# Weight-sum transfers tied to the weight stream, and a fifth raw tile in the last mixed stretch

## The chip, the cores and the metric

The kernel runs on one core of one Trainium2 chip. The metric is the device time of one execution in microseconds (us). Before the change, three runs gave a median of 2760.9 us (2760.19 to 2761.02).

## What is computed

The reference is a two-layer encoder over 272 tokens (16 learned meta tokens and 256 others) of width 2048, all in float32. Cut to what matters:

```
h = RMSNorm(x);  [q|k|v|f|ga|gf] = h @ w_in
a = attention(q, k, v) @ w_attn_br        # per-head norms, rotary
s = Re(2-D DFT(f)) @ w_four
x = x + (sigmoid(ga)*a + sigmoid(gf)*s) @ w_out
x = x + (silu(conv3(RMSNorm(x) @ w_up_gate)) * (RMSNorm(x) @ w_up_val)) @ w_down
```

There are few tokens and many weights, so the kernel is one long stream of weights past a small set of activations. Each float32 product is made of three TensorE products: an operand is split into a rounded high half and the remainder, and high*high, high*low and low*high are added.

## The kernel before, in words

**The stream.** `order` (from line 145) lists all weight groups, and `chunks` all pieces of 512 KB (128 partitions x 1024 float32) in the order of use. For each chunk, `load_raw` (line 198) issues a load on SP's DMA queue into one of `RAW` = 4 raw tiles. `split_w` (line 231) then writes the high half `wh` on ACT (line 237) and the low half `wl` on DVE (line 239); each has three buffers, and a raw tile is free when its `wl` is written. `next_split` (line 275) hands the pair to the matmuls, and splitting runs `LOOK` = 2 chunks ahead. `group` (line 282) does one weight group: 24 matmuls for a chunk, at lines 308 to 310. A chunk is eight 128x128 weight blocks; after every second block, thus four times a chunk, it calls `step` (line 250).

**Side work.** `step` advances generators that were pushed for norms, attention, the Fourier branch and others; what they emit is placed between the matmuls. `step` also counts down a slow generator, `weight_sums` (line 488), first by 120 steps and then by whatever it yields, which is 28. A planner then orders the instructions on each engine by their dependences, their costs and their place in the program; with `tc.keep_in_program_order` an instruction keeps its place.

**The weight sums.** The last layer's down projection treats the first 32 of its 44 feature tiles as a 2x2 block product with seven instead of eight block products (`PRODUCTS`, line 38). Four of them need sums of weight blocks, which stand in DRAM as `ft`. `weight_sums` builds these with DMAs from DRAM to DRAM, issued by GpSimd (POOL): eight rounds of eight transfers of 1 MB. Four of each round copy (line 501), and four add to what is there (line 503). They read only inputs and `ft` itself. `ft` is first read when the products that use it start, late in the last layer.

**Other users of POOL's queue.** POOL runs its queue in order. It also computes the reciprocal square roots of the norms (`pow_half`, line 446, instruction at line 448): `tok` for a token norm, `rk` and `rq` for the keys' and queries' head norms. In the head of the program, layer 0's first groups (`first_groups`, from line 351; matmuls at lines 376 to 378) run the first eight chunks. Their results wait in PSUM for `rstdB`, which comes from `tok` through `ps_nb` (line 527); the keys wait for `rk` through `dk` and `ps_kb` (lines 883 and 886).

**The mixed stretch.** A chunk of the seven products has six matmuls of 512 columns (line 1273), and there are 112 such chunks (`pchunks`). They are mixed into the stream: `due` (line 181) spreads 58 of them over the 48 chunks of the last six up and gate groups of layer 1, and 54 over the 24 chunks of the tail (matmuls at line 1334). `make` (line 1245) prepares the activations for a unit of four product chunks as a pair of halves, `opnd`, in three buffers; it is called at the first chunk of a unit, for the unit after the next.

Of the kernel before, what the change touches and what calls it, by code (L numbers as in the profile page):

```python
# [10 lines left out]
F32 = mybir.dt.float32  # L11
F32R = mybir.dt.float32r
# [4 lines left out]
P = 128  # L17
# [15 lines left out]
CW = 4  # L33
MG = 2
# [98 lines left out]
def encoder_kernel(ctx, tc, xT, params, consts, bmat, cfold, csign, w_fl, w_f64c, w_in, w_abr, w_four, w_f64, w_out, w_up, w_down, w_dn, w_dt, out):  # L133
    nc = tc.nc
    per = ctx.enter_context(tc.tile_pool(name="per", bufs=1))
    wp = ctx.enter_context(tc.tile_pool(name="wp", bufs=3))
# [41 lines left out]
    prods = {0: w_dn[0, 0:NQ], 1: w_dn[0, NQ:KS], 2: w_dn[1, NQ:KS], 3: ft[3], 4: ft[0], 5: ft[1], 6: ft[2]}  # L178
    pchunks = [(prods[p][i], CW) for p in PRODUCTS for i in range(NQ)]
    n_up, n_tail = (FT - KS) // MG * 2 * KT // CW, len(TAIL_ORDER) * (FT - KS) // 2  # L180
    due = lambda t: 58 * t // n_up if t <= n_up else min(58 + (len(pchunks) - 58) * (t - n_up) // (n_tail - 2), len(pchunks))
    chunks, folded, mix = [], set(), {}
    t, done = 0, 0
    for key, chs in order:
        for j, ch in enumerate(chs):
            if key[0] == 1 and (key[1] == "t" or key[1] in ("ug", "uv") and key[2] >= KS // MG):
                mix[key, j] = due(t) - done
                chunks += pchunks[done:due(t)]
                done = due(t)
                t += 1  # L190
            if key[:2] == (0, "s"):
                folded.add(len(chunks))
            chunks.append(ch)
    st = {"raw": 0, "fetch": 0, "next": 0, "grp": 0}
    raws, splits = {}, {}
    RAW, LOOK = 4, 2

    def load_raw(i):
        src, n = chunks[i]
        r = wp.tile([P, CW, MG * P], F32, tag="raw", name=f"raw{i}", bufs=RAW)  # L200
        nc.sync.dma_start(r, src)
        raws[i] = r

    todo = []

    def advance(upto):
        while st["raw"] < min(upto + RAW, len(chunks)):
            load_raw(st["raw"])
            st["raw"] += 1
        while st["fetch"] < min(upto, len(chunks)):  # L210
            i = st["fetch"]
            if i in folded:
                todo.append((i, lambda i=i: fold_w(i)))
            for a in (0, 2) if i <= 3 else (0,):
                todo.append((i, lambda i=i, a=a: split_w(i, a, a + 2 if i <= 3 else CW)))
            st["fetch"] += 1
# [8 lines left out]
    def fold_w(i):  # L225
        r = wp.tile([P, CW, MG * P], F32, tag="wpm", name=f"wpm{i}", bufs=1)
        for o, op in ((0, ALU.add), (2, ALU.subtract)):
            nc.vector.tensor_tensor(r[:, o:o + 2], raws[i][:, 0:2], raws[i][:, 2:4], op=op)
        raws[i] = r

    def split_w(i, a, b, parts="hl"):
        if i not in splits:
            splits[i] = tuple(wp.tile([P, CW, MG * P], F32R, tag=t, name=f"{t}{i}") for t in ("wh", "wl"))
        h, lo = splits[i]
        r = raws[i]
        if "h" in parts:
            nc.scalar.copy(h[:, a:b], r[:, a:b])  # L237
        if "l" in parts:
            nc.vector.tensor_tensor(lo[:, a:b], r[:, a:b], h[:, a:b].bitcast(F32), op=ALU.subtract)  # L239
            if b == CW:  # L240
                del raws[i]
# [167 lines left out]
    small = ctx.enter_context(tc.tile_pool(name="small", bufs=4))  # L409
# [78 lines left out]
    def weight_sums():  # L488
        rows = lambda ap: ap.rearrange("k p c m -> (k p) (c m)")
        for j in range(NQ // 2):  # L490
            a, b = 2 * j, 2 * j + 2
            dst = lambda q: rows(ft[q, a:b])
            w = lambda h, k: rows(w_dn[h, NQ * k + a:NQ * k + b])
            for ops in ((((0, w(0, 0)), (2, w(1, 1)), (3, w(0, 1))), None),
                        (((0, w(1, 0)), (2, w(1, 0))), ALU.add),
                        (((1, None),), None),
                        (((1, w(1, 1)),), ALU.add),
                        (((3, dst(1)),), ALU.add)):
                for q, src in ops[0]:
                    if ops[1] is None:  # L500
                        nc.gpsimd.dma_start(dst(q), dst(0) if src is None else src)
                    else:
                        nc.gpsimd.dma_start(dst(q), src, accum_op=ops[1], max_dma_last_dim=4096)
                    yield 28

    def norm_stats(holder, gap=0):
# [29 lines left out]
    for l in range(DEPTH):  # L536
        last = l == DEPTH - 1
        lo = 14 if last else 0
# [4 lines left out]
        with tc.tile_pool(name=f"mix{l}", bufs=1) as mp:  # L543
# [524 lines left out]
            for i in range(4):  # L1068
# [8 lines left out]
                elif i == 0:  # L1077
                    until(hold, "vt")
                    until(hold, "fold")
                    for t_, n in ((qH, "q1"), (qL, "q2")):  # L1080
                        t = mp.tile([P, NH, T], F32R, tag=n, name=n)
# [25 lines left out]
            for half in range(2):  # L1107
                mH = mL = None
                for kind, i in BRANCH_ORDER[half]:
# [19 lines left out]
                    else:  # L1129
# [7 lines left out]
                        for m in range(MG):  # L1137
                            k = 2 * j + m
                            t_, h_ = tha[i][:, m, lo:T], mH[:, k, lo:T]
# [13 lines left out]
        with tc.tile_pool(name=f"ffn{l}", bufs=1) as fp:  # L1153
# [48 lines left out]
            if last:  # L1202
# [11 lines left out]
                def act(k, n, tk):  # L1214
                    k0, t_ = acts[k >= KX]
                    return t_[:, k - k0:k - k0 + n, tk]
# [24 lines left out]
                def products():  # L1241
                    units = [(p, q) for p in PRODUCTS for q in range(NQ // 4)]
                    made = {}

                    def make(u):
                        if u >= len(units):
                            return
                        p, q = units[u]
                        k1, k2 = 4 * q, NQ + 4 * q
                        s = asum[:, k1:k1 + 4]  # L1250
                        if p == 5:
                            nc.vector.tensor_tensor(s, s, act(k1, 4, tk1), op=ALU.subtract)
                        if p == 2:
                            nc.vector.tensor_tensor(s, s, act(k2, 4, tk1), op=ALU.add)
                        v = {0: act(k1, 4, tk1), 1: act(k2, 4, tk1), 3: act(k2, 4, tk2), 6: act(k1, 4, tk2)}.get(p, s)
                        t_ = fp.tile([P, 2, 4, P], F32R, tag="opnd", name="opnd", bufs=3)
                        split_to(t_[:, 0], t_[:, 1], v)
                        made[u] = t_

                    make(0)  # L1260
                    make(1)
                    usum = wp.tile([P, CW, MG * P], F32, tag="wpm", name="usum", bufs=1).rearrange("p c m -> p (c m)")
                    for n, p in enumerate(PRODUCTS):
                        ps = [psum.tile([P, 512], F32, tag="aux", name=f"ps_p{p}") for _ in range(2)]
                        for i in range(NQ):
                            u = (n * NQ + i) // 4
                            if i % 4 == 0:
                                make(u + 2)
                            wh, wl = (w.rearrange("p c m -> p (c m)") for w in next_split())
                            a, b = made[u][:, 0, i % 4], made[u][:, 1, i % 4]  # L1270
                            for x, w in ((a, wh), (b, wh), (a, wl)):
                                for h in range(2):
                                    nc.tensor.matmul(ps[h], x, w[:, 512 * h:512 * h + 512], start=i == 0 and w is wh and x is a,  # L1273
                                                     stop=i == NQ - 1 and w is wl)
                                if x is b or w is wl:
                                    step()
                                    pump()
                            if i == NQ - 1:
                                for h in range(2):
                                    u_ = usum[:, 512 * h:512 * h + 512]  # L1280
                                    if p == 0:
                                        nc.scalar.copy(u_, ps[h])
                                    if p in (5, 6):
                                        nc.vector.tensor_tensor(u_, u_, ps[h], op=ALU.add)
                                    src = u_ if p in (5, 6) else ps[h]
                                    for t_, c, op in {0: ((0, 0, ALU.add),), 4: ((0, 2, ALU.add), (1, 2, ALU.add)), 5: ((0, 2, ALU.subtract),),
                                                      2: ((0, 2, ALU.add),), 6: ((1, 0, ALU.add), (1, 2, ALU.subtract)),
                                                      1: ((0, 0, ALU.add),), 3: ((1, 0, ALU.add),)}[p]:
                                        add(t_, c + h, src, op)
                            yield  # L1290

                st["products"] = products()
                for i in range(FT // MG):
                    cs = conv_gate(i)
                    ps = group((l, "uv", i), lambda kt: (xHL[:, kt, :, lo2:T],), W2)
# [20 lines left out]
                for b in TAIL_ORDER:  # L1316
# [6 lines left out]
                    for j in range(len(chs)):  # L1323
                        for _ in range(mix.get((k, j), 0)):
                            next(st["products"])
                        wh, wl = (w.rearrange("p (k a) m -> p k (a m)", k=2) for w in next_split())
# [83 lines left out]
```

## Time and profile before

| | |
|---|---|
| median of three runs | 2760.9 us |
| profiled execution | 2756.24 us |
| its span, first to last instruction | 2754.1 us |
| mean granted TensorE clock | 0.966 |
| TensorE (PE) busy | 2573.5 us, 93% |
| VectorE (DVE) busy | 1789.5 us, 65% |
| ScalarE (ACT) busy | 1273.0 us, 46% |
| GpSimd (POOL) busy | 64.6 us, 2% |
| moved by DMA | 591.45 MB, mean 215 GB/s |
| of it on POOL's queue (`q0 software_dynamic`) | 67.11 MB |

PE is the engine that carries the kernel; PEld, its weight loads, overlaps it. The profile cuts the span in 40 slices of 68.9 us and shows in tenths how busy each engine and the 16 DMA engines were. A row of a window gives for a stretch of time the busy us of each engine with its number of instructions behind an x, then the granted TensorE clock, the busy share of the DMA engines and GB/s. A row of waits gives the waiting instruction, what ended the wait, us in total, times, and the longest. `L239` is line 239 of the kernel. DMA shares can come out a little above 1.

### The profile page before, as it was taken

Reading aid. Unit: us, or ns where it says so; the run is one execution under the profiler, and the core shown is the slowest. Engines: PE = TensorE matmul, PEld = TensorE weight load, DVE = VectorE, ACT = ScalarE, POOL = GpSimd, SP = SyncE. Lnnn points to the kernel's source line nnn. Section 1 sums busy time; section 2 is a strip of 40 time slices with the busy share of each in tenths; the row PEclk is TensorE's granted clock in tenths of the full one; section 3 lists DMA queues with packets and bytes.
Section 4 is the critical chain, followed back from the end, with each engine's and each line's share of the span. In section 5 each row is a group of like instructions: output and inputs, shape, how many; then the busy total and the mean of one; then the engine's idle time right before and its main releaser. Section 6 shows DMA issues by size and latency. Waiting matters only on the chain.

```text
span 2754.1 us, 47402 instructions
## 1 busy us (share of the span) xinstructions
PE 2573.5 (93%) x19184; PEld 2488.8 (90%) x19184; DVE 1789.5 (65%) x2846; ACT 1273.0 (46%) x1820; POOL 64.6 (2%) x105
## 2 busy tenths in 40 slices
PE   4274599999999999999999999999999999999999
PEld 4274599999999999999999999999999999988877
DVE  2142478677766665566655888766766666788877
ACT  3131255444544443344444555544554444565655
POOL 1111000000000000000000000000000000000000
PEclk7586799999999999999999999999999999999999
DMA  9999845555566666666654554555545555577787
GB/s 294 294 306 278 223 143 178 188 187 190 185 237 222 222 227 228 220 221 231 229 191 172 181 194 152 186 188 194 194 172 186 187 186 184 199 259 254 259 293 256
DMA packets 158730, 591.45 MB, mean 215 GB/s; under 512 B 18080, under 2 KB 23328, under 8 KB 158000
## 3 DMA queue, kind: packets, MB, share of 16 engines
q1 hardware_dynamic: 147344, 519.19, 54.7%
q0 software_dynamic: 9728, 67.11, 9.2%
q8 instruction: 150, 2.46, 0.4%
q10 hardware_dynamic: 1440, 2.13, 0.2%
q14 instruction: 68, 0.56, 0.1%
HBM read 566.70 MB, written 85.98 MB: 237 GB/s over the span
## 4 chain that ended last, share of the span: by engine, by line
PE 83%; DMA 12%; DVE 2%; issue 1%; POOL 1%; ACT 1%; SPq 0%; ACTq 0%; DVEq 0%; POOLq 0%
DMA ft<-in_w_dn 7%; PE ps_ug L309 6%; PE ps_ug L308 6%; PE ps_ug L310 6%; PE ps_uv L304 6%; PE ps_p L1273 4%; DMA ft<-ft 4%; PE ps_uv L308 3%; PE ps_d L308 3%; PE ps_d L309 3%; PE ps_uv L309 3%; PE ps_uv L310 3%; PE ps_d L310 3%; PE ps_uv L305 3%; PE ps_gf L308 2%; PE ps_gf L309 2%
## 5 line engine op out<-in xcount | busy, mean ns | idle before, releaser
L239 DVE TENSOR_TENSOR wl<-raw,wh 128x1024 fp32r<-128x1024 f32 (+1 forms) x901 | 1093.1, 1218 | 683.6 <-ACT wh L237 678.4
L237 ACT CAST wh<-raw 128x1024 fp32r<-128x1024 f32 (+1 forms) x901 | 938.3, 1044 | 1082.0 <-PE ps_ug L309 194.7
L309 PE MATMUL ps_ug<-xHL,wh 128*128 128x272 f32 (+1 forms) x1408 | 402.3, 286 | 0.0
L308 PE MATMUL ps_ug<-xHL,wh 128*128 128x272 f32 (+1 forms) x1408 | 402.1, 286 | 0.0
L310 PE MATMUL ps_ug<-xHL,wl 128*128 128x272 f32 (+1 forms) x1408 | 401.7, 285 | 0.0
L308 PEld LDWEIGHTS ps_ug<-xHL,wh 128*128 128x128 f32 x1408 | 265.4, 188 | 1.7
L309 PEld LDWEIGHTS ps_ug<-xHL,wh 128*128 128x128 f32 x1408 | 265.4, 188 | 1.0
L310 PEld LDWEIGHTS ps_ug<-xHL,wl 128*128 128x128 f32 x1408 | 264.9, 188 | 0.2 <-DVE wl L239 0.2
L304 PE MATMUL ps_uv<-xHL,wh 128*128 128x512 f32 x704 | 248.9, 395 | 0.1
L309 PE MATMUL ps_d<-gHL,wh 128*128 128x272 f32 x704 | 203.1, 289 | 0.0
L309 PE MATMUL ps_uv<-xHL,wh 128*128 128x272 f32 x704 | 203.1, 288 | 0.0
L308 PE MATMUL ps_uv<-xHL,wh 128*128 128x272 f32 x704 | 202.9, 288 | 0.0
L308 PE MATMUL ps_d<-gHL,wh 128*128 128x272 f32 x704 | 202.9, 288 | 0.0
L310 PE MATMUL ps_uv<-xHL,wl 128*128 128x272 f32 x704 | 202.8, 288 | 0.0
L310 PE MATMUL ps_d<-gHL,wl 128*128 128x272 f32 x704 | 202.7, 288 | 0.0
L305 PE MATMUL ps_uv<-xHL,wl 128*128 128x256 f32 x704 | 197.6, 281 | 0.3
L304 PEld LDWEIGHTS ps_uv<-xHL,wh 128*128 128x128 f32 x704 | 132.3, 188 | 30.3 <-ACT wh L237 0.6
L308 PE MATMUL ps_ga<-xHL,wh 128*128 128x272 f32 (+1 forms) x512 | 148.2, 290 | 0.0
L308 PE MATMUL ps_gf<-xHL,wh 128*128 128x272 f32 (+1 forms) x512 | 147.3, 288 | 0.0
L310 PE MATMUL ps_ga<-xHL,wl 128*128 128x272 f32 (+1 forms) x512 | 146.3, 286 | 0.0
L309 PE MATMUL ps_gf<-xHL,wh 128*128 128x272 f32 (+1 forms) x512 | 146.2, 286 | 0.0
L310 PE MATMUL ps_gf<-xHL,wl 128*128 128x272 f32 (+1 forms) x512 | 146.2, 286 | 0.0
(353 smaller groups left out, 5896.9 us busy)
## 6 DMA issues: line engine op xcount, KB each, us to landing
raw<-in_w_up SPq DMA_DIRECT2D x352, 512.0 KB, 3.5
raw<-in_w_in SPq DMA_DIRECT2D x191, 512.0 KB, 4.1
raw<-in_w_down SPq DMA_DIRECT2D x88, 512.0 KB, 3.5
raw<-in_w_out SPq DMA_DIRECT2D x64, 512.0 KB, 3.5
raw<-ft SPq DMA_DIRECT2D x64, 512.0 KB, 4.6
ft<-in_w_dn POOLq DMA_DIRECT2D x24, 1024.0 KB, 17.4
raw<-in_w_dn SPq DMA_DIRECT2D x48, 512.0 KB, 4.6
raw<-in_w_abr SPq DMA_DIRECT2D x32, 512.0 KB, 3.5
```

Of the source, the lines that this page charges most:

```text
L237: nc.scalar.copy(h[:, a:b], r[:, a:b])
L239: nc.vector.tensor_tensor(lo[:, a:b], r[:, a:b], h[:, a:b].bitcast(F32), op=ALU.subtract)
L304: nc.tensor.matmul(o2, h[:, c, sl], ab, start=kt == 0, stop=False)
L305: nc.tensor.matmul(o, lo[:, c, sl], ab[:, 0, :], start=False, stop=kt == nk - 1)
L308: nc.tensor.matmul(o, h[:, c, sl], a, start=kt == 0, stop=False)
L309: nc.tensor.matmul(o, h[:, c, sl], b, start=False, stop=False)
L310: nc.tensor.matmul(o, lo[:, c, sl], a, start=False, stop=kt == nk - 1)
L1273: nc.tensor.matmul(ps[h], x, w[:, 512 * h:512 * h + 512], start=i == 0 and w is wh and x is a, stop=i == NQ - 1 and w is wl)
```

## The change

There are three edits.

1. In `weight_sums`, each of the 64 transfers is preceded by a one-column copy on POOL (`tick`, 128x1) that reads the low half `wl` of the chunk that was last given to `split_w`. The copy and the transfer both keep their program order. `split_w` notes that low half in `st["wl"]`.
2. In the mixed stretch a fifth raw tile, `raw5`, is taken from the pool of the last layer's feed-forward part. Of each five loads from there on the fifth goes into it, and loads run five ahead. `opnd` has two buffers instead of three, and `make` prepares a unit after the first chunk of the unit before it, rather than two units ahead.
3. `due` spreads 66 instead of 58 product chunks over the up and gate groups, so 46 instead of 54 are left for the tail.

```diff
-    due = lambda t: 58 * t // n_up if t <= n_up else min(58 + (len(pchunks) - 58) * (t - n_up) // (n_tail - 2), len(pchunks))
+    due = lambda t: 66 * t // n_up if t <= n_up else min(66 + (len(pchunks) - 66) * (t - n_up) // (n_tail - 2), len(pchunks))
...
+                if t == 0:
+                    first_mix = len(chunks)
...
-        r = wp.tile([P, CW, MG * P], F32, tag="raw", name=f"raw{i}", bufs=RAW)
+        if i >= first_mix and (i - first_mix) % (RAW + 1) == RAW:
+            r = st["pool"].tile([P, CW, MG * P], F32, tag="raw5", name=f"raw{i}", bufs=1)
+        else:
+            r = wp.tile([P, CW, MG * P], F32, tag="raw", name=f"raw{i}", bufs=RAW)
...
-        while st["raw"] < min(upto + RAW, len(chunks)):
+        while st["raw"] < min(upto + RAW + (upto > first_mix), len(chunks)):
...
+        st["wl"] = lo
         if "l" in parts:
...
                 for q, src in ops[0]:
+                    tick = small.tile([P, 1], F32, tag="tick", name="tick", bufs=1)
+                    tc.keep_in_program_order(nc.gpsimd.tensor_copy(tick, st["wl"][:, 0, 0:1].bitcast(F32)))
                     if ops[1] is None:
-                        nc.gpsimd.dma_start(dst(q), dst(0) if src is None else src)
+                        tc.keep_in_program_order(nc.gpsimd.dma_start(dst(q), dst(0) if src is None else src))
                     else:
-                        nc.gpsimd.dma_start(dst(q), src, accum_op=ops[1], max_dma_last_dim=4096)
+                        tc.keep_in_program_order(nc.gpsimd.dma_start(dst(q), src, accum_op=ops[1], max_dma_last_dim=4096))
                     yield 28
...
-                        t_ = fp.tile([P, 2, 4, P], F32R, tag="opnd", name="opnd", bufs=3)
+                        t_ = fp.tile([P, 2, 4, P], F32R, tag="opnd", name="opnd", bufs=2)
...
                     make(0)
-                    make(1)
...
-                            if i % 4 == 0:
-                                make(u + 2)
+                            if i % 4 == 1:
+                                make(u + 1)
...
                 st["products"] = products()
+                st["pool"] = fp
```

## The prediction

> **What bounds the kernel now.** I read the page's busy slices first, then the chain that ended last, then the same span in three windows.
>
> ```profile
> ## 2 busy tenths in 40 slices
> PE   4274599999999999999999999999999999999999
> ...
> DMA  9999845555566666666654554555545555577787
> ```
> ```profile
> PE 83%; DMA 12%; DVE 2%; issue 1%; POOL 1%; ACT 1%; SPq 0%; ACTq 0%; DVEq 0%; POOLq 0%
> ```
> ```profile
> core 0: us, PE busy (x) PEld busy (x) DVE busy (x) ACT busy (x) POOL busy (x), PEclk, DMA share, GB/s
> 0.00:325.00 325.00, 152.85 (x977) 145.92 (x978) 92.27 (x194) 68.53 (x129) 53.24 (x86) 0.71 1.01 284
> 325.00:2500.00 2175.00, 2173.64 (x16949) 2136.34 (x16948) 1501.47 (x2436) 1055.86 (x1523) 11.34 (x19) 1.00 0.57 198
> 2500.00:2754.10 254.10, 246.99 (x1263) 206.56 (x1261) 195.79 (x218) 148.63 (x168) 0.00 (x0) 1.00 0.79 267
> ```
>
> The chain is PE's work for 83%, and nearly all of its 12% of DMA comes first. From 325 us on PE has no room: it is idle for 1.4 of 2175 us, and for 7.1 of the last 254. All the room lies in the first 325 us, where the DMA engines are full (share 1.01) and PE works less than half the time, at a granted clock of 0.71. Who fills the DMA, and what PE waits for, stand in the transfers and the waits of the head:
>
> ```profile
> q0 software_dynamic: 9668, 66.93, 77.8%
> ```
> ```profile
> raw<-in_w_in SPq DMA_DIRECT2D x40, 512.0 KB, 18.8
> ```
> ```profile
> PE ps_nb L527 <- DVE dg L524: 44.5, 1, 44.5
> PE ps_kb L886 <- DVE dk L883: 42.7, 1, 42.7
> PE ps_f L376 <- ACT wh L237: 37.4, 6, 14.1
> PE ps_q L310 <- DVE wl L239: 24.0, 3, 13.4
> PE ps_ss L839 <- ACT qps L831: 14.8, 2, 14.3
> ```
>
> All 64 weight sums (66.93 of 67.11 MB) run in the head and take 77.8% of the engines, 253 us of 16 engines, though nobody reads `ft` before the last layer. A raw load of 512 KB lands after 18.8 us there; the page has 3.5 for the steady stream:
>
> ```profile
> raw<-in_w_up SPq DMA_DIRECT2D x352, 512.0 KB, 3.5
> ```
>
> The sums hurt in a second way: POOL stands in its queue before a sum that needs an earlier one, and the norms' small work stands behind it. The operand of `rk` was ready at 189.5 us, and `rk` ran at 233.9:
>
> ```profile
> 189.36 0.17 DVE L876 TENSOR_SCALAR kss<-kss 128x6 f32<-128x6 f32 x1
> ```
> ```profile
> 233.85 1.67 POOL L448 TENSOR_TENSOR rk<-kss,mhalf 128x6 f32<-128x6 f32 x1
> ```
>
> **Edit 1, what it takes away.** In the built kernel's order on POOL, the first copy reads the low half of chunk 31 (from zero) and the others follow seven chunks apart (28 steps, four a chunk), the last at chunk 488 of 912. `rk` stands ahead of the first sum, and so does layer 0's first `tok`. How fast PE does the head's work when nothing is late is shown by a full window:
>
> ```profile
> 400.00:425.00 25.00, 25.00 (x204) 25.00 (x202) 19.81 (x49) 14.14 (x27) 0.00 (x0) 1.00 0.45 150
> ```
>
> That is 8.16 matmuls per us, 2.94 us for a chunk of 24. The head's 977 matmuls are then 120 us of work, and 325 - 120 = 205 us are lost, part as idle time and part as half clock after each gap. What stays lost:
>
> ```profile
> 4.49 0.60 PE L376 MATMUL ps_f<-xHL,wh 128*128 128x272 f32 x1 [4.49 <-ACT wh L237]
> ...
> 9.89 0.29 PE L378 MATMUL ps_f<-xHL,wl 128*128 128x272 f32 x1
> ```
> ```profile
> 0.00:25.00 25.00, 10.66 (x47) 9.94 (x48) 7.00 (x16) 8.72 (x19) 7.03 (x23) 0.75 0.91 285
> ```
>
> - The start, 4.5 us, and the first chunk at low clock, 5.4 instead of 2.9 us: 7 us for certain.
> - The first loads. Chunks 0 to 7 and the activations are 4.2 + 2.2 = 6.4 MB: at 285 GB/s 22.5 us, with 3.5 for landing and 2.3 for the split 28.3 (the split's two instructions are in the next rows). PE without waits would want chunk 7 at 9.9 + 6 x 2.94 = 27.5 us. The two are level, so short waits alternate: 5 us, between nothing and all 37.4 of `ps_f`.
> - The chains through `tok`, `rk` and the swap of the heads' rows. In the new order 36 matmuls (4.4 us) stand between the transposes and `ps_nb`, and 66 (8.1 us) between the keys' transposes and `ps_kb`; the chain is 1.7 us on POOL as above, some small DVE steps like the 0.17, and perhaps a `wl` of 1.2 in their way. Late next is `rstdB`, behind constants that load at that time. 8 us for all, between nothing and the 14.8 of `ps_ss`.
>
> ```profile
> L239 DVE TENSOR_TENSOR wl<-raw,wh 128x1024 fp32r<-128x1024 f32 (+1 forms) x901 | 1093.1, 1218 | 683.6 <-ACT wh L237 678.4
> L237 ACT CAST wh<-raw 128x1024 fp32r<-128x1024 f32 (+1 forms) x901 | 938.3, 1044 | 1082.0 <-PE ps_ug L309 194.7
> ```
>
> So 205 - 20 = 185 us go; with the ends, 205 - 7 - 52 = 146, and 205 - 7 = 198.
>
> **Edit 1, what it adds.** 64 copies on POOL and the sums under the steady stream. A one-column copy stands in the trace, like the sums' issue:
>
> ```profile
> L420 POOL COPY raw<-raw 128x1 f32<-128x1 f32 x1 | 0.4, 433 | 0.0
> ```
> ```profile
> L503 POOL DMA_DIRECT2D ft<-in_w_dn x24 | 22.6, 957 | 135.9 <-DMA ft<-ft 118.4 <-DMA ft<-in_w_dn 17.3 <-issue 0.3
> ```
>
> 64 x 0.43 = 28 us, on an engine that is idle for 2690. Behind a waiting copy stand the norms' instructions; the copy waits for a split under way, at most 2.3 us, and its transfer's issue takes 1. There are seven such instructions among the sums (`rq` four times, `tok` twice, `rk` once), each with other groups' matmuls in front of its reader: 1 us, between 0 and 7 x 3.3 = 23. The copy also holds one of three `wl` buffers, which PE holds longer: nothing, unless POOL stands still (a rival below).
>
> A sum that is alone can be seen at the end of the head: the transfers between 318 and 330 us.
>
> ```profile
> raw<-in_w_in SPq DMA_DIRECT2D x3, 512.0 KB, 5.3
> ft<-ft POOLq DMA_DIRECT2D x1, 1024.0 KB, 7.8
> ```
>
> It lands after 7.8 us, and the next comes 7 x 2.94 = 20.6 us after it, so they rarely meet. Raw loads beside it land after 5.3 instead of 3.5. Splitting runs two chunks ahead and four raw tiles rotate, so a load has four chunks, 11.8 us, before its cast is due: cover of 6.5 us. If that cover were gone, each sum would cost the 1.8 us. Over the 64 x 20.6 = 1320 us the sums add 253/1320 = 0.19 to the DMA share. These rows show what PE loses at high shares:
>
> ```profile
> 925.00:1000.00 75.00, 75.00 (x600) 75.00 (x599) 49.01 (x77) 33.45 (x43) 0.00 (x0) 1.00 0.66 232
> 2425.00:2500.00 75.00, 75.00 (x456) 67.03 (x455) 61.71 (x79) 47.88 (x62) 0.00 (x0) 1.00 0.76 255
> 2575.00:2650.00 75.00, 74.27 (x359) 61.22 (x358) 58.51 (x64) 47.29 (x54) 0.00 (x0) 1.00 0.82 279
> 2650.00:2725.00 75.00, 72.68 (x317) 57.95 (x316) 59.38 (x59) 45.23 (x48) 0.00 (x0) 1.00 0.87 293
> ```
>
> Nothing at 0.76, 1% at 0.82, 3% at 0.87. The busiest stage to come is that of 0.66, some 600 us long, then at 0.85. It uses a chunk in 2.94 us where the last rows use one in under 2, so its loads have more time. I take 3 us, between 0 and 3% of 600, 18.
>
> [...]
>
> **Edits 2 and 3.** PE's work is the same; eight product chunks of 1.39 us move out of the tail. The chain shows the first product chunk, the first matmuls of the tail and the last ones:
>
> ```profile
> 2389.19 1.39 PE ps_p L1273 x6
> ```
> ```profile
> 2604.46 2.74 PE ps_t L1334 x12
> ```
> ```profile
> 2744.78 5.64 PE ps_t L1334 x36
> ```
>
> The up groups' part had 106 chunks of 0.524 MB in 215 us, 258 GB/s; it gets 114 in 226, 264 GB/s, under the 279 at which PE lost 1%. The tail had 78 in 146 us, 280 GB/s, and gets 70 in 135, 272. PE's idle time after 2500 us is 7.1 us, of which 3.7 lie behind the last matmul (2750.4 to 2754.1); the fifth raw tile and the lower rate can win at most the other 3.4, and I take 1. Against it stands `opnd` with two buffers:
>
> ```profile
> L1180 DVE TENSOR_TENSOR opnd<-act,opnd x12: 681/685/687, 2073.0 to 2697.3; 128x512 fp32r<-128x512 f32 x12
> ```
>
> Its buffer is free when the last chunk of the unit before is done, and three chunks of cover remain; without cover 27 units x 0.69 = 19 us. Nothing is taken, 19 is the end.
>
> **Sum.** On the profiled execution: 2756.2 - 185 + 1 + 3 - 1 = 2574 us. The median of the runs is 4.7 us above that execution, so 2579.
>
> **Rivals.**
> - Every sum slows the stream by what the raw load is late, 1.8 us: 64 x 1.8 = 115, 2579 - 3 + 115 = 2691. For it speaks the landing of 5.3; against it the cover of 6.5 us and the full PE at share 0.76. 6%.
> - The head stays bound by its own loads, and only POOL's two waits go: 44.5 + 42.7 = 87, 2760.9 - 87 + 3 = 2677. For it: `ps_f` waits for its first loads already at 10 us. Against: its 16 chunks are 8.4 MB, 30 us at 284 GB/s. 6%.
> - The change does not act, because the planner puts the sums elsewhere: its order shows them spread. 1%.
> - Slower: the copies turn the sums into a brake. In a round of eight, two sums wait on POOL for the one right before them (the add to the second block and the add of it to the fourth), 16 in all; the others that wait do so for a sum two or three places back. If a sum lands later than the 20.6 us between two copies, and the 5.9 by which a copy may be late before its `wl` buffer is wanted again, the stream stops for the rest. That eats the gain from 26.5 + 185/16 = 38 us of landing on; at 40 us 16 x 13.5 = 216 is lost, and the time 2760.9 - 185 + 216 = 2792. For it speaks that sums did take long in the head; against it that the longest landing on `ft`, among several at once, is 25.2. 3%.
>
> ```profile
> DMA to landing us min/median/max: 3.2/7.0/25.2
> ```
>
> **The numbers.** The forecast has 84%; its own range is 2760.9 - 198 - 3 = 2560 to 2760.9 - 146 + 18 = 2633. I give 2562 to 2640 for 8 in 10. A measurement of this kernel tells 0.2% from no change, 5.5 us. Faster: 0.95 (forecast, first two rivals). Same: 0.01. Slower: 0.04.
>
> **What would show it.** Right: PE full from the second slice on, sums 20 us apart up to some 1500 us, raw landings near 4 us in the head, `ps_nb` and `ps_kb` without waits of 40 us. Wrong: PE idle in short pieces every 20 us (first rival), `ps_f` still waiting 37 us (second), DVE's `wl` waiting for POOL (third), new waits for `opnd` after 2388 us. The largest term, 185, is wrong if PE idles on something that the sums hid so far.

## The result and the profile after

The changed kernel takes 2564.5 us in the median of four runs (2562.35 to 2570.13), the kernel before 2761.0 beside it (2760.19 to 2761.37). The ratio is 0.9292, with a 95% interval of 0.9276 to 0.9308: faster by 7.1%, 196.5 us. The forecast of 2579 was 14.5 us too high, inside its range. The profiled execution took 2564.79 us over a span of 2562.9.

The page of the changed kernel, its busy slices and the chain:

```profile
PE   9999999999999999999999999999999999999999
...
PEclk9999999999999999999999999999999999999999
DMA  7556768788888888888766665555555555787887
```
```profile
PE 46%; DVE 0%; issue 0%
```

PE is full from the first slice on, and DMA has left the chain (which follows only 46% of the span here). The DMA engines, full in the first slices before, now carry the sums beside the stream from the second slice to the 24th (they go out from 109.7 to 1509.8 us). Next are PE's waits over the whole span (without those of `ps_f` for its first loads), and these first loads on PE's timeline:

```profile
PE ps_f L773 <- DVE qp L840: 2.0, 1, 2.0
PE ps_s L350 <- DVE wl L245: 1.0, 2, 0.6
PE ps_ss L847 <- DVE sqm L950: 0.9, 1, 0.9
PE ps_pt L1024 <- ACT wh L242: 0.8, 1, 0.8
PE ps_fa L607 <- DVE E L586: 0.6, 1, 0.6
PE ps_pv L1046 <- DVE PL L1038: 0.4, 1, 0.4
```
```profile
4.50 0.59 PE L382 MATMUL ps_f<-xHL,wh 128*128 128x272 f32 x1 [4.50 <-ACT wh L242]
...
6.56 0.59 PE L382 MATMUL ps_f<-xHL,wh 128*128 128x272 f32 x1 [0.33 <-ACT wh L242]
```

`ps_nb` and `ps_kb`, 87 us before, are gone from the list, and so are `ps_q` and most of `ps_ss`. Of the 37.4 us for the first loads 4.83 are left, 4.50 of them the start.

The stretches of the changed kernel, with the columns of the windows before:

```profile
0.00:25.00 25.00, 20.17 (x138) 19.74 (x139) 19.07 (x40) 20.73 (x45) 2.86 (x17) 1.00 0.87 308
0.00:134.00 134.00, 128.57 (x1007) 127.72 (x1008) 97.15 (x204) 72.41 (x137) 9.76 (x26) 1.00 0.63 209
134.00:1500.00 1366.00, 1360.52 (x10870) 1356.33 (x10870) 930.21 (x1558) 633.95 (x927) 67.98 (x140) 1.00 0.77 247
900.00:975.00 75.00, 75.00 (x598) 75.00 (x598) 38.58 (x47) 26.19 (x25) 3.52 (x8) 1.00 0.87 285
1050.00:1125.00 75.00, 75.00 (x599) 75.00 (x599) 48.09 (x73) 33.67 (x43) 3.96 (x8) 1.00 0.89 273
```

The work that took 325 us is done in some 130. The last two rows are among the busiest under the sums, with a DMA share of 0.87 and 0.89, and PE loses nothing there. Over the 1366 us of the spread sums it is idle for 5.5.

To place gains and losses, I use the tile views. Each row ends with the first and last start of its group, in us; between first starts lie stages with the same matmuls in each kernel. First the kernel before, then the changed one:

```profile
L308 PE MATMUL ps_ga<-xHL,wh x512: 277/286/373, 339.7 to 1950.6; 128*128 128x272 f32 x86, 128*128 128x258 f32 x85
```
```profile
L308 PE MATMUL ps_ug<-xHL,wh x1408: 277/285/488, 729.0 to 2582.5; 128*128 128x272 f32 x88, 128*128 128x258 f32 x88
```
```profile
L314 PE MATMUL ps_ga<-xHL,wh x512: 277/285/393, 143.8 to 1762.7; 128*128 128x272 f32 x86, 128*128 128x258 f32 x85
```
```profile
L314 PE MATMUL ps_ug<-xHL,wh x1408: 278/285/487, 537.3 to 2406.1; 128*128 128x272 f32 x88, 128*128 128x258 f32 x88
```

The head ends at 143.8 instead of 339.7 (-195.9); the rest of layer 0's mixing, `ps_ga` to `ps_ug`, takes 393.5 instead of 389.3 (+4.2). The table carries this through, with the experiments of the next section. A is start to `ps_ga`, B `ps_ga` to `ps_ug`, C `ps_ug` to the first `ps_d`, D from there to layer 1's first `ps_uv` (all of layer 1's mixing lies in it), E the mixed stretch, from the first `ps_p` to the last start of `ps_t<-wh,tH`. Between D and E are 358.6 or 358.7 us in every kernel.

| kernel | A | B | C | D | E | median, us |
|---|---|---|---|---|---|---|
| before | 339.7 | 389.3 | 290.1 | 1011.3 | 360.9 | 2761.0 |
| changed | 143.8 | 393.5 | 290.1 | 1015.3 | 357.3 | 2564.5 |
| edit 1 alone | 145.8 | 395.1 | 290.1 | 1017.7 | 363.1 | 2573.0 |
| edits 2 and 3 alone | 342.8 | 389.4 | 290.1 | 1011.4 | 353.9 | 2752.0 |
| order kept, no copies | 146.5 | 414.9 | 354.8 | 1019.8 | 353.8 | 2652.3 |
| no sums | 144.9 | 388.9 | 290.1 | 1011.3 | 353.8 | 2553.3 |
| a sum every 7 steps | 151.0 | 478.3 | 290.0 | 1012.1 | 357.3 | 2656.5 |
| a sum every 14 steps | 145.8 | 409.2 | 292.2 | 1012.0 | 357.3 | 2579.8 |
| before, roots off POOL | 289.4 | 408.1 | 290.0 | 1013.3 | 362.0 | 2727.8 |
| first sum at step 500 | 145.3 | 388.6 | 290.0 | 1012.1 | 357.3 | 2559.0 |
| four raw tiles | 143.3 | 392.8 | 290.1 | 1015.5 | 359.1 | 2568.5 |
| 58 product chunks | 145.3 | 391.1 | 290.0 | 1016.7 | 357.3 | 2565.7 |
| copy's tile padded | 143.6 | 396.0 | 290.1 | 1017.5 | 354.4 | 2565.0 |
| step 500 and padded | 143.5 | 388.9 | 290.1 | 1012.8 | 354.4 | 2556.4 |

Stages are those of one profiled execution. Between kernels with the same work in a stage they scatter: A from 143.3 to 145.8, B with spread sums from 391.1 to 396.0 (without sums 388.6 to 389.4), D from 1015.3 to 1017.7; C and E agree within 0.2.

### The profile page after: what moved, and what is told of

It reads as the page before. It is cut to its first block, busy times and chain, and to the rows that moved or that the text cites. A ratio compares the mean times of both kernels' runs of the same rounds, so it can differ in the third digit from the quotient of the medians.

```text
span 2562.9 us, 47568 instructions
## 1 busy us (share of the span) xinstructions
PE 2548.2 (99%) x19184; PEld 2469.9 (96%) x19184; DVE 1786.1 (70%) x2846; ACT 1273.3 (50%) x1820; POOL 79.7 (3%) x169
## 3 DMA queue, kind: packets, MB, share of 16 engines
q0 software_dynamic: 9728, 67.11, 10.5%
## 6 DMA issues: line engine op xcount, KB each, us to landing
ft<-in_w_dn POOLq DMA_DIRECT2D x24, 1024.0 KB, 11.8
```

## The experiments

Diffs are against the changed kernel, but for "roots off POOL", which is against the kernel before. Ratios are to the kernel before on the same chip, with a 95% interval.

**The parts alone.** Edit 1 alone takes edits 2 and 3 back:

```diff
-    due = lambda t: 66 * t // n_up if t <= n_up else ...
+    due = lambda t: 58 * t // n_up if t <= n_up else ...
...
-        while st["raw"] < min(upto + RAW + (upto > first_mix), len(chunks)):
+        while st["raw"] < min(upto + RAW, len(chunks)):
...
-                        t_ = fp.tile([P, 2, 4, P], F32R, tag="opnd", name="opnd", bufs=2)
+                        t_ = fp.tile([P, 2, 4, P], F32R, tag="opnd", name="opnd", bufs=3)
```

> Edit 1 alone: the kernel before with the one-column copies and the fixed order of the sums; four raw tiles, three operand buffers and 58 products in the up groups as before. The theory that the sums' place in the head is all of the gain gives the changed kernel's 2564.5 us plus the 3.5 us of idle time that the tail of the kernel before has: 2568, between 2564 and 2572. If the fifth raw tile and the new mix carry more than that, the time is above 2575.

Measured: 2572.98 us, ratio 0.9308 (0.9296 to 0.9321). Edit 1 alone takes 190.8 us off the 2763.75 of the kernel before beside it. It came out 5 us slower than expected: E is 2.2 us *longer* than before, though all sums are over by then.

Edits 2 and 3 alone leave `weight_sums` as it was:

```diff
-                    tick = small.tile([P, 1], F32, tag="tick", name="tick", bufs=1)
-                    tc.keep_in_program_order(nc.gpsimd.tensor_copy(tick, st["wl"][:, 0, 0:1].bitcast(F32)))
...
-                        tc.keep_in_program_order(nc.gpsimd.dma_start(...))
+                        nc.gpsimd.dma_start(...)
```

> Edits 2 and 3 alone: fifth raw tile, two operand buffers, 66 products in the up groups; the sums stay without copies and without a fixed order, so that the planner puts them at the start. The theory gives 2761 less the tail's 3.5 us: 2757.5, between 2754 and 2762. A rival, that the new mix is worth tens of us, gives under 2740.

Measured: 2751.99 us, ratio 0.9959 (0.9945 to 0.9972), a gain of 11.8 us in the medians, more than the range allowed. In the stages, E goes from 360.9 to 353.9, 7.0 us, twice what the changed kernel shows there (357.3). The rest of the 11.8 isn't located: A is 3.1 us longer in the profiled execution. So something in edit 1 costs E 3.4 us with the other edits and 2.2 without them; the last experiments go after it.

**What the copies are for.** The sums kept in program order, but without the copies:

```diff
-                    tick = small.tile([P, 1], F32, tag="tick", name="tick", bufs=1)
-                    tc.keep_in_program_order(nc.gpsimd.tensor_copy(tick, st["wl"][:, 0, 0:1].bitcast(F32)))
```

> The changed kernel without the one-column copies; the transfers keep their program order. On POOL one sum then stands at the very start, 20 in a row stand behind the queries' second reciprocal root of layer 0, and 42 behind the feed-forward part's token norm. The rk and tok of the head are free of the sums. Theory that the DMA engines' time is what the sums took: in the head of the kernel before, raw loads got 25.3 MB in 325 us, 78 GB/s, beside sums in a row; 62 sums in a row at some 5 us each are 310 us in which the stream gets 78 to 130 instead of 178 GB/s, so 85 to 175 us are lost again: 2650 to 2740. Theory that only the norms' place behind the sums in POOL's queue cost time: no more than 20 us above the changed kernel, under 2585.

Measured: 2652.33 us, ratio 0.9599 (0.9581 to 0.9616), at the near end of what the bandwidth theory gave. The head is as short as in the changed kernel (146.5), and the time is lost later. Its window and two of PE's waits:

```profile
600.00:890.00 290.00, 251.32 (x1796) 244.28 (x1796) 148.07 (x231) 100.62 (x132) 21.71 (x31) 0.92 0.95 302
```
```profile
PE ps_ug L314 <- ACT wh L242: 15.5, 6, 4.7
PE ps_uv L314 <- ACT wh L242: 12.0, 5, 3.4
```

The sums run in a bunch wherever POOL is free to issue them. Share 0.95 at 302 GB/s, raw loads landing after up to 30.0 us, PE at 251 of 290 us and a granted clock of 0.92. Against the kernel before, the loss is 25.6 us in B, 64.7 in C and 8.5 in D: what the copies do is spread the sums; where they begin alone does not do it.

The sums left out: four of the seven block products then read plain blocks of `w_dn`.

```diff
-    prods = {0: ..., 1: ..., 2: ..., 3: ft[3], 4: ft[0], 5: ft[1], 6: ft[2]}
+    prods = {0: ..., 1: ..., 2: ..., 3: w_dn[1, 0:NQ], 4: w_dn[0, 0:NQ], 5: w_dn[0, NQ:KS], 6: w_dn[1, NQ:KS]}
...
-    slow[1] = weight_sums()
```

> The changed kernel without any weight sum and without the copies; the four products that read sums read plain weight blocks of the same size instead, so four of the seven block products of the last down projection are wrong, and all else is the same work. This is the floor that spreading can reach. The theory that the spread sums cost the 8 us by which the changed kernel's stages lag behind (4.5 in layer 0's attention, 4.0 in layer 1's) gives 2556, between 2553 and 2560. The rival that each sum still slows the stream by 1.8 us gives 2450. If the 8 us come from something else, the time is that of the changed kernel, 2562 to 2567.

Measured: 2553.32 us, ratio 0.9241 (0.9229 to 0.9254). That is the floor: 64 spread sums and their copies cost 11.1 us in all, 0.17 us each. By stage they cost 4.6 us in B, 4.0 in D and 3.5 in E, and nothing in C, where the DMA share of the changed kernel is highest (0.84, against 0.71 in B and 0.72 in D). The head is the same with and without them.

**Was it POOL's queue or the bandwidth?** In the kernel before, the reciprocal roots moved off POOL, so that no norm waits behind a sum, with the sums where they were:

```diff
-        nc.gpsimd.tensor_tensor(out, src, mhalf[:, :n], op=ALU.pow)
+        nc.scalar.activation(out, src, AF.Sqrt)
+        nc.vector.reciprocal(out, out)
```

> The kernel before with the norms' reciprocal roots taken from POOL to ACT and DVE (a square root and a reciprocal), so that nothing that PE waits for stands behind the sums in POOL's queue; the sums stay at the start. Ten table loads on ACT may cost 10 to 15 us. Theory that both causes count: the two long waits of 44.5 and 42.7 us go, part of them comes back because the raw loads then share the engines with the sums for longer: 2690 to 2740. Theory that POOL's queue was the whole cause: 2570 to 2590. Theory that only the bytes count: 2750 to 2775.

Measured: 2727.76 us, ratio 0.9894 (0.9874 to 0.9914), within what was expected if both causes count. PE's waits and its window of the head:

```profile
PE ps_f L376 <- ACT wh L237: 36.7, 6, 13.1
PE ps_fa L600 <- issue: 22.8, 1, 22.8
PE ps_q L310 <- DVE wl L239: 19.2, 1, 19.2
PE ps_pt L1017 <- DVE pn L1008: 17.1, 2, 16.7
PE ps_ss L840 <- ACT qps L832: 14.8, 2, 14.2
PE ps_nb L528 <- DVE dg L525: 10.8, 1, 10.8
```
```profile
0.00:325.00 325.00, 185.83 (x1218) 178.96 (x1218) 122.22 (x266) 91.14 (x173) 47.33 (x82) 0.78 1.02 295
```

`ps_kb` is gone and `ps_nb` down from 44.5 to 10.8, 76 us of waits, and the time falls by 30. Other waits take their place (`issue` is a wait for which the profile shows no releaser), and the DMA engines stay full (1.02). The head, A, is 50.3 us shorter, but only 59.06 MB of the sums' 67.11 are moved by its end; the rest goes on beside B, which is 18.8 us longer. So the two waits on POOL, the largest of the list before, were a part of the loss and not the bulk of it. The experiment is not quite clean: the roots' new place has a price of its own, on ACT ten table loads of 1.28 us each in its profile (seven at line 448, three at line 1000, 12.8 us), which may be part of the new waits (`ps_fa` above all).

**How close the sums may stand.** A sum every 7 or 14 steps instead of 28, and the first sum after 500 steps instead of 120:

```diff
-                    yield 28
+                    yield 7
```
```diff
-                    yield 28
+                    yield 14
```
```diff
-    slow = [120, None]
+    slow = [500, None]
```

> The changed kernel with a copy and a sum every 7 steps instead of 28, a sum each 5.1 us: the sums run from about 90 to 430 us. The theory of shared DMA engines: a sum takes 4.0 us of all engines, raw loads 1.85 us for each chunk of 2.94 us, so the engines are asked for 4.0/5.1 + 1.85/2.94 = 1.41 of their time, and the stretch of 330 us becomes some 465: 2564 + 135 = 2700, between 2660 and 2740. The copies then show the brake: a sum that waits on POOL for an earlier one holds the next copy and with it a low half, and DVE waits for POOL. [...]

> The changed kernel with a copy and a sum every 14 steps, a sum each 10.3 us, from about 90 to 750 us. Asked of the DMA engines: 4.0/10.3 + 1.85/2.94 = 1.02 without the prefold's transfers, so the engines are just full. Theory of shared engines: 5 to 40 us above the changed kernel, 2570 to 2605, most of it at the start of layer 0's attention part and in layer 0's up groups, where the prefold adds loads. If a lone sum is what counts and not the share, the cost is that of the changed kernel, the same 8 us for 64 sums: 2560 to 2568.

> The changed kernel with the first copy after 500 steps instead of 120, so that the sums begin behind layer 0's attention, at about 390 us, and end at about 1800 us, still ahead of their first use. The theory that 4.5 us are lost where the sums run beside layer 0's attention part gives 2560, between 2557 and 2562. If those 4.5 us come from the attention part itself (its small work on DVE and ACT is close together), the time stays 2562 to 2567.

Measured, in this order: 2656.48 us, ratio 0.9635 (0.9616 to 0.9655); 2579.77, 0.9354 (0.9339 to 0.9370); 2559.02, 0.9281 (0.9267 to 0.9295). At 7 steps, 44 us less was lost than I had set as the likeliest value, and the time is just under the range; the other two are within theirs. The window, waits and the transfers of B at 7 steps:

```profile
250.00:350.00 100.00, 81.91 (x600) 81.26 (x599) 60.21 (x106) 38.31 (x62) 15.82 (x31) 0.90 0.98 291
```
```profile
PE ps_gf L316 <- DVE wl L245: 26.4, 4, 12.8
...
DVE wl L245 <- POOL tick L507: 11.1, 3, 7.5
```
```profile
ft<-in_w_dn POOLq DMA_DIRECT2D x22, 1024.0 KB, 12.4
```
```profile
L507 POOL COPY tick<-wl x64: 173/200/1178, 110.3 to 551.0; 128x1 f32<-128x1 f32 x64
```

The last row gives the copies' first and last start: on average 440.7/63 = 7.0 us apart, and not the 5.1 (7 x 2.94 / 4) that I had reckoned with, since the stream that spaces them is slowed itself. At 14 steps they come 11.0 us apart (111.6 to 807.6). Sums now land after 12.4 us, the DMA share is 0.98, and B is 89 us longer. Here DVE's `wl` waits for a copy on POOL, 11.1 us of three waits, which it does not in the changed kernel: the brake exists, and is the smaller part of the loss.

With the first sum later, B is 388.6 us, that of the kernel without sums. The windows of layer 0's attention, first of the changed kernel, then with the sums later:

```profile
143.00:168.00 25.00, 23.23 (x185) 22.64 (x184) 22.75 (x60) 13.72 (x30) 2.87 (x3) 1.00 0.48 168
...
243.00:268.00 25.00, 24.37 (x195) 24.02 (x194) 18.86 (x34) 11.27 (x18) 1.13 (x2) 1.00 0.67 197
268.00:293.00 25.00, 24.52 (x196) 24.17 (x195) 19.71 (x38) 11.53 (x18) 1.45 (x2) 1.00 0.87 264
```
```profile
143.00:168.00 25.00, 25.00 (x203) 24.91 (x203) 22.73 (x60) 14.75 (x31) 1.79 (x1) 1.00 0.37 125
...
243.00:268.00 25.00, 25.00 (x203) 25.00 (x202) 20.42 (x38) 12.04 (x18) 0.00 (x0) 1.00 0.59 198
268.00:293.00 25.00, 25.00 (x203) 25.00 (x202) 18.82 (x33) 12.04 (x18) 0.00 (x0) 1.00 0.60 203
```

The loss sits in short idle pieces of the attention part, at shares (0.48, 0.67) at which the feed-forward part loses nothing. DVE is close to full there (22.75 of 25 us in the first window). D, through nearly all of which sums now run, kept 0.8 of its 4.0 us, so it seems to be a matter of which sum meets which step. For the one gap of D that PE's waits show in the changed kernel, these are DVE's step in the kernel before, the same step and PE in the changed kernel, the sum ahead of it, and the windows around it:

```profile
1572.77 0.73 DVE L849 TENSOR_TENSOR qs<-qs,cst 128x544 f32<-128x544 f32 x1 [0.22 <-DMA qs<-qp]
```
```profile
1383.20 0.72 DVE L857 TENSOR_TENSOR qs<-qs,cst 128x544 f32<-128x544 f32 x1 [1.86 <-DMA qs<-qp]
```
```profile
1388.40 0.39 PE L773 MATMUL ps_f<-hA,wh 128*128 128x276 f32 x1 [2.02 <-DVE qp L840]
```
```profile
1370.15 0.95 POOL L511 DMA_DIRECT2D ft<-in_w_dn  x1 [0.26 <-issue]
```
```profile
1370.00:1380.00 10.00, 10.00 (x86) 10.00 (x85) 8.29 (x14) 6.22 (x10) 1.22 (x3) 1.00 0.99 247
1380.00:1390.00 10.00, 7.99 (x64) 7.62 (x63) 7.30 (x11) 4.11 (x7) 0.00 (x0) 0.96 0.64 206
1390.00:1400.00 10.00, 10.00 (x77) 9.88 (x77) 7.79 (x10) 5.27 (x8) 0.00 (x0) 0.87 0.69 235
```

A sum goes out at 1370; the share is 0.99. Under it, the small transfer that swaps the heads' rows (`qs<-qp`) lands late, and DVE's chain waits 1.86 us for it, where it waited 0.22 before. PE stands for 2.02 (0.4 in the kernel before, 0.3 with the first sum later), and then does 77 matmuls in 10 us instead of 86 at a granted clock of 0.87. The weights were not late here: a transfer in the middle of a chain was, which no raw tile covers.

**The mixed stretch.** Four raw tiles with the new `due` and `opnd`; and five with the old `due`:

```diff
-        if i >= first_mix and (i - first_mix) % (RAW + 1) == RAW:
+        if False:
...
-        while st["raw"] < min(upto + RAW + (upto > first_mix), len(chunks)):
+        while st["raw"] < min(upto + RAW, len(chunks)):
```
```diff
-    due = lambda t: 66 * t // n_up if t <= n_up else ...
+    due = lambda t: 58 * t // n_up if t <= n_up else ...
```

> The changed kernel with four raw tiles in the mixed stretch instead of five; two operand buffers and 66 products stay. If the fifth raw tile is what took the tail's idle time away, the 3.5 us or more come back: 2568 to 2572, and PE waits for wl and wh in the tail again. If moving eight products out of the tail did it, the time is that of the changed kernel, 2562 to 2567.

> The changed kernel with 58 instead of 66 products in the up groups; the fifth raw tile and the two operand buffers stay. If the mix did it, 2568 to 2572; if the fifth raw tile did, 2562 to 2567.

Measured: 2568.51 us, ratio 0.9301 (0.9288 to 0.9313), and 2565.68, 0.9294 (0.9281 to 0.9306). The medians hardly part, but E does: 363.1 with neither, 359.1 with the new `due` alone, 357.3 with the fifth tile alone, 357.3 with both. The fifth tile alone does all of it, the new `due` most, and the two don't add. With four raw tiles PE's own waits for `wh` and `wl` did not come back in that stretch; those of its weight loads did, 2.3 us.

Then the 3.5 us that edit 1 costs in E. In the built kernels the copy's 4-byte tile takes 32 bytes of each partition and moves tiles made later, `opnd` and `tH` among them: they begin 32 bytes past a multiple of 64 (at bytes 220000 and 181664 of a partition), where without the copies (219968 and 181632), or with a copy's tile of 64 bytes (220032 and 181696), they begin on one. So the tile was padded, alone and together with the later start:

```diff
-                    tick = small.tile([P, 1], F32, tag="tick", name="tick", bufs=1)
+                    tick = small.tile([P, 16], F32, tag="tick", name="tick", bufs=1)[:, 0:1]
```

> The changed kernel with the copy's tile 64 bytes long in each partition instead of 4; the copy itself stays one column. The tile of 4 bytes takes 32 in memory, and moves every later tile by 32, so that the operands opnd and tH of the last stretch start at 32 beyond a multiple of 64; with 64 bytes they start at a multiple of 64 again. Theory that this offset is why matmuls of 512 columns start 0.2333 us apart in every kernel with copies and 0.2270 in those without: the mixed stretch becomes 353.8 instead of 357.3 us, and the time 2561, between 2558 and 2563, with 0.227 between matmuls. If the copies or the late sums slow them in another way, 357.3 us and 0.233 stay.

> The changed kernel with the first copy after 500 steps and the copy's tile of 64 bytes. If the two gains add, 2564.5 - 4.5 - 3.5 = 2556, between 2553 and 2558, within 3 us of the kernel without any sums. If they don't add, 2559 to 2562.

Measured: 2564.95 us, ratio 0.9286 (0.9274 to 0.9299), and 2556.40, 0.9259 (0.9247 to 0.9272). Padding brings E from 357.3 to 354.4, 2.9 of the 3.5 us; alone it doesn't show in the median, and in the profiled execution B and D came out 2.5 and 2.2 us longer, within their scatter. The product matmuls in the tile views (shortest, median and longest ns), first changed, then padded:

```profile
L1280 PE MATMUL ps_p<-wh,opnd x448: 389/396/399, 2201.3 to 2552.7; 128*128 128x512 f32 x150
```
```profile
L1280 PE MATMUL ps_p<-wh,opnd x448: 387/389/399, 2205.8 to 2554.3; 128*128 128x512 f32 x150
```

Those that read `opnd` go from 396 to 389 ns, below the 392 of the kernels without copies. The range of 2558 to 2563 for the padded kernel was missed. Both edits together give the best version, 8 us below the changed kernel's median and 3 above the kernel without sums; on the same chip, its slowest run (2559.42) is under the fastest of the padded kernel (2562.28).

## Why the prediction was right, and what it had wrong

**The head.** Right in cause, mis-sized in what stays. 205 us of loss less 20 gave 185; the stage gives 195.9, so 9 stay. The 7 us of the start and the first chunk are there. The two other items, 5 us of first loads and 8 of chains, came to 1: in the head `ps_f` waits 0.33 us beside the start and `ps_fa` 0.6 (the 0.9 of `ps_ss` come behind it, in B). I had costed the first loads as level with PE and the chains from waits measured under full DMA engines; with 308 GB/s in the first 25 us instead of the 285 that I took, the loads were ahead. This is the larger part of the error: 11 of the 14.5 us.

**The sums under the stream.** 3 us and 1 for POOL, against some 8 us in B and D. The size is within its range (0 to 18 and 0 to 23); the place was wrong. I looked at the feed-forward part with the highest share, where the loss is nil at 0.89, above the share at which I had expected 3%. The loss is in the attention parts, by a late swap in the one piece that I followed; the other pieces of B were not traced to their cause. Of the copies' price, 0.43 us each was too high:

```profile
L507 POOL COPY tick<-wl x64: 175/183/1045, 109.6 to 1509.3; 128x1 f32<-128x1 f32 x64
```

64 x 0.18 = 12 us, on an engine with that to spare; nobody waits for one at 28 steps. The row gives the spacing as well, 1400/63 = 22 us, where 20.6 was forecast.

**Edits 2 and 3.** 1 us forecast, 3.6 in E, and 7.0 where the copies' tile is not in the way. I had allowed 3.4 at most, the idle time of PE that the windows show in that stretch, as if its busy time were all work. That was the failed step: PE's weight loads (PEld) waited longer for late halves than PE stood idle. In the mixed stretch of the kernel before their waits come to 7.9 us (6.7 in the tail's matmuls, 1.2 in the products'), with edits 2 and 3 alone to 0.6. The longest row of them:

```profile
PEld ps_t L1334 <- DVE wl L239: 5.6, 8, 1.0
```

The difference is close to the 7.0 us gained. No wait for `opnd` came up.

**The median.** I added 4.7 us because the median stood above the profiled execution; in the changed kernel the two are level (2564.5 and 2564.8). Without that step the forecast would be 2574.

The four: +11 from the head, -4 to -5 from the sums, +2.6 from edits 2 and 3, +5 from the median, together some 14.

**The rivals.** *Each sum slows the stream by 1.8 us* (2691): fell; 64 sums and their copies cost 11.1 us, 0.17 each. The cover is the likely reason, though no run varies the buffers under the sums: raw loads of this part land after 5.0 us instead of 3.5, and PE stays full.

```profile
raw<-in_w_up SPq DMA_DIRECT2D x150, 512.0 KB, 5.0
```

Raw loads land later beside sums, by that row and by the up to 30.0 us under the bunched ones; how the DMA engines divide their time between the two queues no run here shows. *The head stays bound by its own loads* (2677): fell, at 143.8 us. The experiment with the roots bounds it from the other side: freeing POOL alone gives 30 us. *The copies as a brake* (2792): not at 28 steps, where the sums' four groups of transfers land after 7.0 to 12.7 us in the median; it showed at 7 steps, 11.1 us of waits, where it is a minor part. *No effect*: fell.

## What to carry to other kernels

Background transfers that nobody needs soon were cheap here under the compute-bound part, at a spacing above their landing time of 7.0 to 12.7 us: one of 1 MB each 22 us was nearly free (0.17 us each), one each 11 us cost 15 us more, one each 7 us 92. A small instruction that reads a tile of the stream, here a copy of 0.18 us, spaces them without a clock. And a long wait in the list is no price: two waits of 87 us together were worth 30, because the DMA engines stayed full (share 1.02) and other waits took their place.

## What the runs showed of the hardware

- **A matmul's pace went with where its tiles lie.** Twelve product matmuls of 512 columns take 2.80 us in the kernels with the 4-byte copy tile, and 2.75 in those without; twelve of the tail take 2.79 and 2.72. These rows of the chain that ended last (start, us, and the matmuls behind the x) are of the changed kernel, of edits 2 and 3 alone, and of the padded kernel:

```profile
2515.68 2.80 PE ps_p L1280 x12
2518.49 2.79 PE ps_t L1342 x12
```
```profile
2703.76 2.75 PE ps_p L1278 x12
2706.51 2.72 PE ps_t L1340 x12
```
```profile
2517.81 2.75 PE ps_p L1280 x12
2520.56 2.80 PE ps_t L1342 x12
```

  Padding mended it for `ps_p`, whose 672 matmuls make up the 2.9 us of E (672/12 x 0.05 = 2.8), and not at all for `ps_t`. From the first to the last start of `ps_t<-wh,tH` the tail takes 131.2 us in the changed kernel, 129.9 padded and 128.9 with edits 2 and 3 alone; the 1.3 us that padding brings are about what the 46 product chunks mixed into it gain (276/12 x 0.05 = 1.2). So with `opnd` and `tH` both moved to a multiple of 64 bytes, `ps_p` got faster and `ps_t` did not. In the built kernels `tH` and `tL` begin on a multiple of 128 without the copies (181632 and 193920) and 64 past one when padded (181696 and 193984); whether that is what slows `ps_t` was not run, and stays open.

- **The granted clock fell to 0.50 behind a gap of 2.02 us.** In the changed kernel PE has no matmul for 2.02 us up to 1388.40; the granted clock in windows of 1 us is 1.00 up to 1389, 0.50 from 1390 to 1392 and 1.00 again from 1393. In the kernel before a gap of the same 2.02 us ends at 171.21; there it is 0.50 from 173 to 176, and 1.00 from 177.

- **The granted clock of the profile does not show the slow start.** It says 1.00 for the first 25 us, while the matmuls of the first chunk start 0.22 us apart (4.89, 5.12, 5.34 in PE's timeline), against 0.12 from 10.27 us on (10.27, 10.40, 10.53, 10.65).
